# First block of a hybrid encoder layer: four single k-tiles, x split ahead of its weights, h's rows later, and plain units with the rounded halves first

## The chip, the cores and the metric

The kernel runs on one core of one Trainium2 chip. The metric is the device time of one execution in microseconds (us). The median of three runs of the kernel before is 1040.02 us (1039.77 to 1040.2).

The core has five engines with a queue each: TensorE (PE in the profile; its weight loads are PEld), VectorE (DVE), ScalarE (ACT), GpSimd (POOL) and SyncE (SP), which here only issues DMAs. Each engine works through its own queue in order; a semaphore holds an instruction until what it reads is there or the buffer that it writes is free.

## The reference

All in float32: x is 256 tokens by 2048 features, one layer.

```python
xn = rms_norm(h, norm1_g[l])
proj = jnp.einsum('bsd,dn->bsn', xn, w_in[l])
q, k, v, ga, gg = jnp.split(proj, ...)          # 1024, 1024, 1024, 1024, 1024 columns
...                                              # rope, differential attention: att
u = ga * jax.nn.sigmoid(gg)
u = causal_depthwise_conv(u, conv_w[l], conv_b[l])   # 31 taps
u = jax.nn.silu(layer_norm(u, conv_ln_g[l], conv_ln_b[l]))
h = h + jnp.einsum('bsm,md->bsd', jnp.concatenate([att, u], axis=-1), w_out[l])
hn = rms_norm(h, norm2_g[l])
a, bu = hn @ w_gate[l], hn @ w_up[l]             # 5632 columns each
h = h + (jax.nn.silu(a) * bu) @ w_down[l]
```

## The kernel before

**Three products for one.** A float32 matrix product is made of products of rounded halves. Each operand t becomes hi = t rounded to the matmul's type (fp32r) and lo = t - hi, and the product is xhi·whi + xlo·whi + xhi·wlo. ScalarE makes hi (`round_chunk`, L342 for weights; `split_scaled`, L243 for x), VectorE makes lo (`split_chunk`, L351; L244). The token side is the stationary operand, in two halves m of 128 tokens; the weights stream past, 512 columns a matmul.

**Chunks.** The work is one long list `chunks`. A chunk is some k-tiles (128 rows) of a weight matrix; a block is all chunks that add into one pair of accumulators. In the first block a k-tile is 128 x 512 floats, 256 KB, and of x 128 x 256 floats, 128 KB. A chunk normally has two k-tiles; in the first block `XPARTS` (L54) cuts the chunks: before, one, one, then seven of two. `multiply` (L363) runs the 6 matmuls per k-tile: for every k-tile and m the two with whi (L381, L382), then a turn for the side work (`resume`), then all with wlo (L387).

**Order.** The order on each queue is the order in which Python emits the instructions. `run_chunks` (L474) emits for chunk t what is to stand ahead of its matmuls: in the first block the parting (load, rounding, low half) of chunk t + 1, afterwards that of t + 2 and the rounding of t + 3. Loading chunk c first calls `before[c]`, which puts other work ahead of its weights. Four buffers (`raw`, RAW_BUFS) take loaded weights, so SP sends the weights of chunk n + 4 only when chunk n has its low half; four buffers each take the rounded and the low halves.

- x lies transposed in DRAM with the gains in front. Its first k-tile (`head`) and its second are sent by ACT's queue; the rest by `x_load` on SP's, ahead of the weights of the same chunk.
- `x_part` splits x. Before, only that of the first k-tile stands in `before[0]`; the others were emitted by the generator `x_rest` (L532), one part per chunk, at the turn in the middle of chunk t for chunk t + 1. There the cast of chunk t + 1's weights had been emitted already.
- `h_load` sends x's rows (two pieces of 512 KB for each m, 2 MB in all), which are needed for the sum of squares and, much later, the residual. `H_FROM` (L58) is the chunk from which on a piece goes ahead of each chunk's weights: before, the sixth to the ninth.
- After x's parts `x_rest` squares the rows in four groups (L541, L517), and sets `normed`, for which the first block's epilogue `glu_done` (L562) and the late constants (L185) wait.

**Plain units.** The feed-forward products are blocks of two kinds of chunk. A pair of k-tiles goes through seven products instead of eight (`multiply_pair`); the other k-tiles are plain units of two k-tiles (`multiply_two`, L1106): for k-tile i and token half m the products with whi (L1115 with the activations' hi, L1116 with their lo), a turn, then the products with wlo (L1120). The activations' low halves are made by VectorE (`transposed`, L959, for the down projection).

Of the kernel before, what the change touches and what calls it, by code (L numbers as in the profile page):

```python
# [22 lines left out]
NM = S // P  # L23
# [27 lines left out]

WARM = 17

XPARTS = (range(0, 1), range(1, 2)) + tuple(range(k, k + 2) for k in range(2, 16, 2))  # L54

CONV_BLOCKS = (2, 2, 2, 2)

H_FROM = 5  # L58

AHEAD = 2  # L60
ROUND_AHEAD, MINUS_AHEAD = 3, 5
# [53 lines left out]
def tile_block(  # L115
# [40 lines left out]
    def x_load(ks, queue):  # L156
        i, k = divmod(ks[0], HK)
        n = len(ks)
        queue.dma_start(out=halves_of_x[i][:, k : k + n].rearrange("p k s -> p (k s)"),
                        in_=xt[:, NR + ks[0] * S : NR + (ks[0] + n) * S])  # L160
# [24 lines left out]
    def late_constants():  # L185
        late_loads()
        while not normed:
            yield
        yield from lag(16)
        act.mul(cols[:, AT["sg"] : AT["sg"] + 2], cols[:, AT["sg"] : AT["sg"] + 2], 1.0 - LAMBDA_INIT)  # L190

        act.mul(gb[:, 0, :], gb[:, 0, :], 1.0 / math.sqrt(DH))
        hd = DH // 2
        for i, key in enumerate("qk"):
            for m in range(NM):
                t = pre.tile([P, 2, DH], F32, tag=f"gcs{key}{m}", name=f"gcs{key}{m}", bufs=1)
                pool.tensor_tensor(t[:, 0, :], rt[:, m, 0, :], gb[:, i, :], ALU.mult)
                pool.tensor_tensor(t[:, 1, :hd], rt[:, m, 1, :hd], gb[:, i, hd:], ALU.mult)
                pool.tensor_tensor(t[:, 1, hd:], rt[:, m, 1, hd:], gb[:, i, :hd], ALU.mult)
                gcs[key, m] = t  # L200
        lp = pre.tile([P, 2, DH], F32, tag="att", name="lp", bufs=4)
        for i in range(2):
            pool.tensor_tensor(lp[:, i, :], lamv[:, 2 * i, :], lamv[:, 2 * i + 1, :], ALU.mult)
        yield from lag(4)
        dve.tensor_reduce(ls, lp, AX.X, ALU.add)
# [19 lines left out]
    halves = {}  # L225
# [25 lines left out]
    def start(gen):  # L251
        running.append(gen)
# [42 lines left out]
    before = {}  # L295
# [230 lines left out]
    def x_part(ks):  # L526
        for k in ks:
            xT[k] = lhs_pair("x", k)
            src = halves_of_x[k // HK][:, k % HK] if k else head[:, NR:]
            split_scaled(xT[k], src, col("g1", k) if k > 1 else head[:, AT["g1"] + k : AT["g1"] + k + 1])  # L530

    def x_rest():  # L532
        for part in XPARTS[1:]:
            x_part(part)
            yield
            yield
        for c in range(D // N):
            while len(h_loaded) <= c // 2 * NM + 1:
                yield
            for m in range(NM):  # L540
                square_sum(h[m][:, c * N : (c + 1) * N], ss1[m][:, c : c + 1])  # L541
            yield
        for m in range(NM):
            ss = small.tile([P, 1], F32, tag="ss1", name="ss1")
            dve.tensor_reduce(ss, ss1[m], AX.X, ALU.add)
            rsqrt_mean(rstd1[m], ss, D, EPS)
        yield
        normed.append(True)
# [557 lines left out]
    def multiply_two(c):  # L1106
        while not c["ready"](c):
            resume()
        hi, lo, plain = c["hi"], c["lo"], c["plain"](c)
        qs = (Q3, QX) if c["kind"] == "u" else (Q2, Q4)  # L1110

        def first_half(m, i):
            ms = slice(m * P, (m + 1) * P)
            ps = sum_bank(c, qs[m])
            pe.matmul(ps, plain[i][0][:, ms], hi[:, i, :], start=i == 0 and bool(c["first"].get(qs[m])), stop=False)  # L1115
            pe.matmul(ps, plain[i][1][:, ms], hi[:, i, :], start=False, stop=False)  # L1116

        def second_half(m, i):
            ms = slice(m * P, (m + 1) * P)
            pe.matmul(sum_bank(c, qs[m]), plain[i][0][:, ms], lo[:, i, :], start=False,  # L1120
                      stop=i == 1 and bool(c["last"].get(qs[m])))

        if c is chunks[-1]:
            for m in range(NM):
                for half in (first_half, second_half):
                    for i in range(2):
                        half(m, i)
                if m == 0:
                    start(c["done"](c["sums"]))
                    resume()  # L1130
            return
        for i in range(2):
            for m in range(NM):
                first_half(m, i)
        resume()
        for m in range(NM):
            for i in range(2):
                second_half(m, i)
        resume()
        if c["done"]:  # L1140
            start(c["done"](c["sums"]))
# [151 lines left out]
            down_block(g, n)  # L1293
        j0 += nb

    for c, part in enumerate(XPARTS[2:], 2):
        before[c] = lambda part=part: x_load(part, sp)
    before[0] = lambda: (x_part(XPARTS[0]), start(x_rest()))
    for i in range(2 * NM):
        x_first = before.get(H_FROM + i, lambda: None)  # L1300
        before[H_FROM + i] = lambda i=i, x_first=x_first: (x_first(), h_load(i))
    before[len(XPARTS) + 1] = lambda: start(late_constants())
    run_chunks()


# [35 lines left out]
```

## Time and profile before

| | |
|---|---|
| median of three runs | 1040.02 us |
| the profiled execution's own time | 1041.07 us |
| its span, first to last instruction | 1039.2 us |
| granted TensorE clock, mean over the span | 0.998 |
| HBM read, mean rate | 248.80 MB, 247 GB/s with the writes |
| bytes moved in the first 40 us | 14.46 MB, 362 GB/s |
| last matmuls begin / last VectorE work ends | 1034.3 / 1035.7 us |

The profile lists for each engine what it did and what ended its idle time. A line of the view in order of time is: start in us, duration in us, engine, source line, operation, out<-in, shapes, count, and in brackets the idle time before it with what ended it. A line of the waits is: engine, tile and line that waited, what it waited for, us in total, times, longest. In the list of DMA issues, KB are 1024 bytes, and the last number is the us from issue to landing. Matmuls overlap: one is listed with 0.39 us, but the next starts 0.23 us after it, so paces are read from starts. The last 4 us are the epilogue of the last block and its store, which the change does not touch.

### The profile page before, as it was taken

How to read it: one execution, taken by the hardware profiler on the slowest of the kernel's cores; microseconds unless marked ns; L12 is line 12 of the kernel's file. 1: busy time of each engine (PE TensorE's matmuls, PEld its weight loads, DVE VectorE, ACT ScalarE, POOL GpSimd, SP SyncE). 2: the span in 40 equal slices, each digit the busy share in tenths (PEclk: the TensorE clock that was granted, in tenths of full speed). 3: DMA queues.
4: the chain of work that ended last, by engine and by line, in shares of the span. 5: the costliest groups of instructions: out<-in, count | busy, mean ns of one | idle time of the engine just before them, and what ended most of it. 6: DMA issues, size and time to landing. Idle time of an engine off the chain costs nothing.

```text
span 1039.2 us, 13042 instructions
## 1 busy us (share of the span) xinstructions
PE 1030.1 (99%) x4641; PEld 850.3 (82%) x4641; DVE 862.3 (83%) x1086; ACT 685.6 (66%) x864; POOL 155.4 (15%) x198
## 2 busy tenths in 40 slices
PE   8999999999999999999999999999999999999998
PEld 6888888888888888788888888888888888888886
DVE  5599989898546699999978789999896697998983
ACT  5855568766856567777556567776765666767761
POOL 0040133411100101001002120010001121101021
PEclk9999999999999999999999999999999999999999
DMA  9867766676566669898889998987969999879896
GB/s 357 302 202 211 238 206 213 187 211 176 163 201 231 230 215 281 241 323 240 257 246 298 257 306 267 309 229 249 307 187 285 300 271 331 235 243 298 250 249 129
DMA packets 65777, 258.05 MB, mean 248 GB/s; under 512 B 7344, under 2 KB 8624, under 8 KB 58288
## 3 DMA queue, kind: packets, MB, share of 16 engines
q1 hardware_dynamic: 48656, 201.34, 53.5%
q0 software_dynamic: 16768, 55.58, 28.2%
q8 instruction: 36, 0.59, 0.2%
q10 hardware_dynamic: 288, 0.29, 0.1%
q14 instruction: 29, 0.24, 0.1%
HBM read 248.80 MB, written 8.39 MB: 247 GB/s over the span
## 4 chain that ended last, share of the span: by engine, by line
PE 95%; DVE 2%; ACT 1%; issue 1%; DMA 1%; POOL 0%; SPq 0%; DVEq 0%
PE q L1116 11%; PE q L1120 11%; PE q L1115 11%; PE acc L387 11%; PE acc L382 11%; PE acc L381 11%; PE q L1094 9%; PE q L1096 8%; PE q L1095 8%; PE ps_a L922 1%; DMA raw<-in_wts_dram 1%; PE ps_s L731 1%; PE ps_o L809 0%; DVE y L596 0%; PE ps_h L859 0%
## 5 line engine op out<-in xcount | busy, mean ns | idle before, releaser
L342 ACT CAST whi<-raw 128x1024 fp32r<-128x1024 f32 (+1 forms) x261 | 270.3, 1046 | 105.1 <-PE acc L382 42.0
L351 DVE TENSOR_TENSOR wlo<-raw,whi 128x1024 fp32r<-128x1024 f32 (+1 forms) x173 | 209.0, 1218 | 72.9 <-ACT whi L342 71.4
L381 PE MATMUL acc<-whi,lhi 128*128 128x512 f32 x416 | 164.7, 396 | 1.5 <-ACT lhi L243 1.4
L382 PE MATMUL acc<-whi,llo 128*128 128x512 f32 x416 | 162.8, 391 | 0.7 <-DVE llo L244 0.7
L1077 DVE TENSOR_TENSOR wl<-wt,wh 128x2048 fp32r<-128x2048 f32 x58 | 132.7, 2287 | 20.6 <-ACT wh L1072 20.6
L1068 ACT CAST wh<-wb 128x1536 fp32r<-128x1536 f32 x58 | 86.0, 1483 | 87.5 <-PE q L1095 49.1
L346 POOL DMA_DIRECT2D wlo<-in_wts_dram x74 | 65.0, 889 | 510.4 <-ACT wlo L345 483.6
L1115 PE MATMUL q<-whi,chi 128*128 128x512 f32 x320 | 124.7, 390 | 0.0
L1116 PE MATMUL q<-whi,clo 128*128 128x512 f32 x320 | 124.6, 389 | 0.0
L1072 ACT CAST wh<-wt 128x2048 fp32r<-128x2048 f32 x58 | 110.4, 1904 | 18.5 <-DVE wt L1063 18.4
L1094 PE MATMUL q<-wh,fhi 128*128 128x512 f32 x280 | 109.2, 390 | 0.4 <-DVE sum L1199 0.4
L1096 PE MATMUL q<-wl,fhi 128*128 128x512 f32 x280 | 109.0, 389 | 0.0
L1095 PE MATMUL q<-wh,flo 128*128 128x512 f32 x280 | 109.0, 389 | 0.0
L596 DVE SCALAR_TENSOR_TENSOR y<-upad,cw,y 128x256 f32<-128x256 f32 x240 | 100.8, 488 | 5.3 <-ACT y L589 5.3
L1076 DVE TENSOR_TENSOR wl<-wb,wh 128x1536 fp32r<-128x1536 f32 x58 | 101.6, 1752 | 2.3 <-ACT wh L1068 2.3
L387 PE MATMUL acc<-wlo,lhi 128*128 128x512 f32 x368 | 101.4, 397 | 0.2 <-DVE wlo L351 0.2
L381 PEld LDWEIGHTS acc<-whi,lhi 128*128 128x128 f32 x416 | 78.5, 189 | 18.5 <-ACT lhi L243 1.8
L382 PEld LDWEIGHTS acc<-whi,llo 128*128 128x128 f32 x416 | 78.5, 189 | 17.3 <-DVE llo L244 1.2
L1120 PE MATMUL q<-wlo,chi 128*128 128x512 f32 x320 | 86.9, 393 | 0.0
L387 PEld LDWEIGHTS acc<-wlo,lhi 128*128 128x128 f32 x368 | 68.9, 189 | 14.6 <-DVE wlo L351 0.6
L345 ACT ACTIVATE wlo<-raw 128x1024 fp32r<-128x1024 f32 x74 | 78.1, 1056 | 0.0
L1061 DVE TENSOR_TENSOR wt<-wb 128x1024 f32<-128x1024 f32 x58 | 70.8, 1221 | 1.8 <-DMA wb<-in_wts_dram 1.3
(224 smaller groups left out, 1732.5 us busy)
## 6 DMA issues: line engine op xcount, KB each, us to landing
raw<-in_wts_dram SPq DMA_DIRECT2D x259, 512.0 KB, 5.6
wb<-in_wts_dram SPq DMA_DIRECT2D x57, 1024.0 KB, 8.1
wlo<-in_wts_dram POOLq DMA_DIRECT2D x74, 512.0 KB, 9.3
lod<-in_wts_dram POOLq DMA_DIRECT2D x14, 512.0 KB, 5.8
out_dram<-sum POOLq DMA_DIRECT2D x22, 256.0 KB, 7.2
h<-in_x_dram SPq DMA_DIRECT2D x4, 512.0 KB, 8.4
out_dram<-h POOLq DMA_DIRECT2D x8, 256.0 KB, 4.7
xt<-in_xt_dram SPq DMA_DIRECT2D x7, 256.0 KB, 6.9
```

What stands on the lines that cost most here:

```text
L342: act.copy(c["hi"], c["raw"])
L351: dve.tensor_tensor(c["lo"], c["raw"], c["hi"].bitcast(F32), ALU.subtract)
L381: pe.matmul(ps[m], xhi[:, ms], hi[:, j, :], start=c["first"] and j == 0, stop=False)
L382: pe.matmul(ps[m], xlo[:, ms], hi[:, j, :], start=False, stop=False)
L387: pe.matmul(ps[m], xhi[:, ms], lo[:, j, :], start=False, stop=c["last"] and j == nk - 1)
L1077: dve.tensor_tensor(c["lo"][:, :4], c["t"], c["hi"][:, :4].bitcast(F32), ALU.subtract)
L1094: pe.matmul(ps, fhi[:, f, p, :], c["hi"][:, w], start=bool(first), stop=False)
L1095: pe.matmul(ps, flo[:, f, p, :], c["hi"][:, w], start=False, stop=False)
L1096: pe.matmul(ps, fhi[:, f, p, :], c["lo"][:, w], start=False, stop=bool(last))
L1115: pe.matmul(ps, plain[i][0][:, ms], hi[:, i, :], start=i == 0 and bool(c["first"].get(qs[m])), stop=False)
L1116: pe.matmul(ps, plain[i][1][:, ms], hi[:, i, :], start=False, stop=False)
L1120: pe.matmul(sum_bank(c, qs[m]), plain[i][0][:, ms], lo[:, i, :], start=False, stop=i == 1 and bool(c["last"].get(qs[m])))
```

## The change

- `XPARTS` becomes four single k-tiles and six pairs: ten chunks in the first block instead of nine. x's third and fourth k-tile and their weights are loaded, rounded and multiplied singly.
- `x_part` of every chunk moves into `before[c]`: x is split on ScalarE and VectorE ahead of the same chunk's weights, no longer at the turns of `x_rest`.
- h's rows go ahead of chunks 8 to 11 (counted from 0) instead of 5 to 8. `x_rest` starts with the tenth chunk and holds only the squares.
- The late constants start ahead of chunk 12 instead of chunk 10. One chunk of that shift is the new chunk of the first block.
- In `multiply_two` the products of the rounded activations with whi come first for all four (i, m), then those of the low halves. The last chunk of all keeps its order.

```diff
-XPARTS = (range(0, 1), range(1, 2)) + tuple(range(k, k + 2) for k in range(2, 16, 2))
+XPARTS = tuple(range(k, k + 1) for k in range(4)) + tuple(range(k, k + 2) for k in range(4, 16, 2))
...
-H_FROM = 5
+H_FROM = 8
...
     def x_rest():
-        for part in XPARTS[1:]:
-            x_part(part)
-            yield
-            yield
         for c in range(D // N):
...
-        def first_half(m, i):
+        def first_half(m, i, halves=(0, 1)):
             ms = slice(m * P, (m + 1) * P)
             ps = sum_bank(c, qs[m])
-            pe.matmul(ps, plain[i][0][:, ms], hi[:, i, :], start=i == 0 and bool(c["first"].get(qs[m])), stop=False)
-            pe.matmul(ps, plain[i][1][:, ms], hi[:, i, :], start=False, stop=False)
+            for e in halves:
+                pe.matmul(ps, plain[i][e][:, ms], hi[:, i, :], stop=False,
+                          start=i == e == 0 and bool(c["first"].get(qs[m])))
...
-        for i in range(2):
-            for m in range(NM):
-                first_half(m, i)
+        for e in range(2):
+            for i in range(2):
+                for m in range(NM):
+                    first_half(m, i, (e,))
         resume()
...
-    for c, part in enumerate(XPARTS[2:], 2):
-        before[c] = lambda part=part: x_load(part, sp)
-    before[0] = lambda: (x_part(XPARTS[0]), start(x_rest()))
+    for c, part in enumerate(XPARTS):
+        before[c] = lambda c=c, part=part: (x_load(part, sp) if c > 1 else None, x_part(part))
+    before[H_FROM + NM - 1] = lambda part=XPARTS[H_FROM + NM - 1]: (x_load(part, sp), x_part(part), start(x_rest()))
     for i in range(2 * NM):
         x_first = before.get(H_FROM + i, lambda: None)
         before[H_FROM + i] = lambda i=i, x_first=x_first: (x_first(), h_load(i))
-    before[len(XPARTS) + 1] = lambda: start(late_constants())
+    before[H_FROM + 2 * NM] = lambda: start(late_constants())
```

## The prediction

> **What bounds the kernel now.** I read the page first (spans and busy shares), then TensorE's waits, then the first 32 us in order of time, then the DMA landings.
>
> ```profile
> span 1039.2 us, 13042 instructions
> PE 1030.1 (99%) x4641; PEld 850.3 (82%) x4641; DVE 862.3 (83%) x1086; ACT 685.6 (66%) x864; POOL 155.4 (15%) x198
> ```
>
> TensorE is busy for all but 9 us. So only three things can make this kernel shorter: fewer matmuls, a shorter idle time of TensorE, or a better clock. The change keeps the matmuls. The waits name nearly all of the idle time that is not the start or the tail:
>
> ```profile
> PE acc L381 <- ACT lhi L243: 1.4, 1, 1.4
> PE ps_warm L149 <- POOL neghalf L143: 1.4, 1, 1.4
> PE acc L382 <- DVE llo L244: 0.7, 1, 0.7
> PE q L1116 <- DVE llo L959: 0.6, 2, 0.4
> PE q L1094 <- DVE sum L1199: 0.4, 1, 0.4
> PE acc L387 <- DVE wlo L351: 0.2, 1, 0.2
> ```
>
> The change touches three of these rows: L381 and L382 (x's halves late in the first block) and L1116 (an activation's low half late in a plain unit). Together they are 2.7 us. The clock adds to that. Three equal stretches of the first block follow; the columns are length, busy us of PE, PEld, DVE, ACT and POOL with counts, then TensorE's granted clock, DMA share and GB/s:
>
> ```profile
> 5.60:9.00 3.40, 2.95 (x12) 2.00 (x12) 1.45 (x3) 1.26 (x3) 0.00 (x0) 1.00 0.98 372
> 9.00:12.40 3.40, 1.74 (x6) 1.23 (x7) 2.92 (x4) 3.12 (x6) 0.00 (x0) 1.00 1.03 399
> 12.40:15.80 3.40, 3.40 (x9) 2.60 (x8) 3.08 (x6) 1.92 (x4) 0.00 (x0) 0.51 1.01 371
> ```
>
> After a stretch in which PE was busy for 2.95 of 3.40 us the clock stayed at 1.00; after one with 1.74 of 3.40 it was 0.51 for the next 3.40 us. The half clock costs about 1.7 us, which no wait shows. The DMA engines are full (share about 1) throughout: the first block is bound by its feed. These are the matmuls and, below them, ScalarE's work:
>
> ```profile
> 5.38 0.61 PE L381 MATMUL acc<-whi,lhi 128*128 128x512 f32 x1
> ...
> 29.02 0.39 PE L381 MATMUL acc<-whi,lhi 128*128 128x512 f32 x1
> ...
> 31.74 0.39 PE L381 MATMUL acc<-whi,lhi 128*128 128x512 f32 x1
> ```
>
> ```profile
> 4.73 1.12 ACT L342 CAST whi<-raw 128x512 fp32r<-128x512 f32 x2
> 5.76 0.51 ACT L243 ACTIVATE lhi<-xt,head 128x256 fp32r<-128x256 f32 x1
> 8.40 1.04 ACT L342 CAST whi<-raw 128x1024 fp32r<-128x1024 f32 x1 [2.14 <-DMA raw<-in_wts_dram]
> 9.36 0.91 ACT L243 ACTIVATE lhi<-xt,cols 128x256 fp32r<-128x256 f32 x2
> ...
> 15.74 1.05 ACT L342 CAST whi<-raw 128x1024 fp32r<-128x1024 f32 x1 [1.35 <-DMA raw<-in_wts_dram]
> ...
> 25.41 1.05 ACT L342 CAST whi<-raw 128x1024 fp32r<-128x1024 f32 x1 [1.36 <-DMA raw<-in_wts_dram]
> ...
> 28.12 0.62 ACT L517 ACTIVATE junk<-h 128x512 f32<-128x512 f32 x1
> ...
> 31.01 2.93 ACT L342 CAST whi<-raw 128x1024 fp32r<-128x1024 f32 x3
> ```
>
> The last chunk of the first block runs from 29.02 to 31.74: 2.72 us for 12 matmuls, 0.2267 us each. The block has 16 k-tiles of 6 matmuls, so 96 x 0.2267 = 21.76 us at full pace. It takes 31.74 - 5.38 = 26.36. **4.6 us are lost**: 2.1 in the two waits, 1.7 to the clock, and about 0.8 in the first slow matmul and in the starts after the waits. That is the pool from which the first half of the change can draw.
>
> **The change, part by part.** I number chunks as the new kernel does: c0 to c3 one k-tile, c4 to c9 two, c10 the first of the next block; wN is cN's weights. A k-tile of weights is 256 KB, one of x 128 KB, each piece of h's rows 512 KB.
>
> *The feed.* ScalarE's waits on the DMA are landings. From 15.74 to 25.41 three chunks landed with 256 KB of x, 512 of h and 512 of weights each: 3840 KB in 9.67 us, 397 KB per us. From 8.40 to 15.74 it was three chunks' x and weights (3 x 768 KB) and one piece of h: 2816 KB, 384 KB per us. So a landing goes by the bytes issued ahead of it. Counted from the code's order and sizes, the old kernel has issued 797 KB through w1 (x0 with the gains is 157), 1565 through its third chunk (8.40) and 4381 through its sixth (15.74). In the new order w3 ends at the same 1565 KB, so it lands at 8.40. Then w4 (2333) lands at 8.40 + 768/384 = 10.40, w5 at 12.4, w6 at 14.4, w7 at 16.4. The first h comes only ahead of w8: w9 (7197 KB) lands at 15.74 + 2816/397 = 22.83, w10 (8221) at 25.41. That is the same byte order as before with 2048 KB of h moved behind the chunks that were starved.
>
> Does the smaller first load leave the queue empty? w4 needs a raw buffer back:
>
> ```profile
> 6.08 0.33 SPq L333 DMA_DIRECT2D raw<-in_wts_dram  x1
> ```
>
> ```profile
> raw<-in_wts_dram SPq DMA_DIRECT2D x1, 512.0 KB, 3.2
> ```
>
> The first row is when the old fifth weight load went out, once the first chunk's low half was made; w4 will go at the same time. The second is a load in a quiet stretch (56 to 62 us): 3.2 us from issue to landing. 6.08 + 3.2 = 9.3 is earlier than 10.40, so the bytes ahead bind, not the issue. A gap of some tenths is possible.
>
> *Order on ScalarE and VectorE.* Now x's halves are queued ahead of the weights' cast. In the old order x's tiles waited behind the cast of 8.40 although nothing shows them waiting for their own data (9.36 follows the cast at once). A single k-tile costs ScalarE 0.51 + 1.12/2 = 1.07 us against 1.36 us of matmuls, so it keeps up. Two more casts and subtractions in all cost nothing, hidden in ScalarE's waits for the DMA (2.14 and 1.35 in the rows above); without that cover, 2 x 0.1 us. c1 to c3 then run without a wait: w3 at 8.40 gives a cast by 8.97, and c3 is wanted at 5.38 + 1.6 + 2 x 1.36 = 9.7 (c0 takes 1.36 and some 0.25 for its slow first matmul). c4 is wanted at 11.07; its cast ends at 10.40 + 1.05 = 11.45, so **a new wait of 0.45 us**. From then on PE needs 2.72 us per chunk and the feed 768/384 = 2.0, so the lead grows. In the stretch 9.0 to 12.4 PE would be busy for 2.95 of 3.40, the very number after which the clock held: **the half clock goes**.
>
> *h's squares.* ScalarE squares h in groups of four; 28.12 to 31.01 is one group, 2.9 us. In the old program the cast of the next block's first chunk stood ahead of the group; now it stands behind. w9's cast ends at 22.83 + 1.05 = 23.9, the squares at 26.8, c10's cast at 27.8; PE wants c10 at 5.38 + 0.25 + 21.76 + 0.45 = 27.84. So 0 to 0.3 us, I take 0.1. SP also sends h's last pieces, and then the late constants (764 KB by the code's shapes), between the next weight loads: w11 lands at 25.41 + 1024/397 = 28.0 against a start of c11 at 30.6, w12 at 28.0 + 1276/397 = 31.2 against 33.3. Both casts (1.05) fit.
>
> Sum of the first half: c10 starts at 27.9 instead of 31.74, **3.8 us gained** (bounds: 4.4 with no new wait, 2.5 with the new wait at 1.7).
>
> *Plain units.* Four matmuls with the rounded halves come ahead of the four with the low halves. The two waits of L1116 in order of time, and VectorE beside them:
>
> ```profile
> 984.52 0.48 PE L1115 MATMUL q<-whi,lhi 128*128 128x512 f32 x1
> 985.37 0.50 PE L1116 MATMUL q<-whi,llo 128*128 128x512 f32 x1 [0.38 <-DVE llo L959]
> ...
> 987.99 0.39 PE L1115 MATMUL q<-whi,lhi 128*128 128x512 f32 x1
> ...
> 990.29 1.07 PE L1120 MATMUL q<-wlo,lhi 128*128 128x512 f32 x4
> ```
>
> ```profile
> 984.63 0.69 DVE L959 TENSOR_TENSOR llo<-ac,lhi 128x512 fp32r<-128x512 f32 x1
> ...
> 987.83 0.69 DVE L959 TENSOR_TENSOR llo<-ac,lhi 128x512 fp32r<-128x512 f32 x1
> 988.43 1.22 DVE L351 TENSOR_TENSOR wlo<-raw,whi 128x1024 fp32r<-128x1024 f32 x1
> ```
>
> The first low half is there at 985.32; four rounded matmuls last to 984.52 + 0.91 = 985.43: no wait. The second is late by VectorE's own queue: 988.52, and the weights' low half at 989.65, so L1120 starts at 989.7 instead of 990.29: what is late next is that subtraction. **0.6 us gained** (0.57 by the waits, 0.75 if VectorE moves up too). The other units show no wait and keep their count of matmuls; they change accumulators after each matmul instead of after two, which the rows price at nothing (bounds 0 and 0.01 us a unit).
>
> *Does the gain reach the end?* VectorE is the only other engine that is full later, while the convolution's taps run:
>
> ```profile
> DVE t L708 <- ACT qn L701: 2.7, 1, 2.7
> ```
>
> This is its one wait between 147 and 170 us, on a chain that starts at a matmul's result. So VectorE had 2.7 us to spare and moves with PE. I take the whole gain.
>
> Sum: 3.8 + 0.6 = 4.4 us from the profiled execution's own 1041.07 gives 1036.7; the median of the runs is 1.05 lower, 1040.02, and **1035.6** there.
>
> **The rivals.**
>
> *The half clock stays.* By the Trainium skill, "TensorE: Matmul & The Clock Gate", Part 1, the gate looks through a free-running window of about 3.4 us and throttles after an idle one. No run here shows an idle window before the drop: PE was busy for 1.74 of 3.40. By that rule the stall would not be the cause. If the drop is not tied to that stall, or if w4 is a microsecond late (1.95 of 3.40 busy, near the 1.74 that dropped), 1.7 us of the gain stay away, in the second case 1.0 more: 1037.3 to 1038.3. For: the threshold lies anywhere between 1.74 and 2.95. Against: 2.95 held.
>
> *The conv stage takes it back.* The 0.2 us wait at L387 for wlo says VectorE was once just in time. If its run were paced by itself alone, PE would wait there for all of the 3.8 us: 1039.4. The 2.7 us wait above speaks against it.
>
> *Each transfer pays its fixed time in series.* 512 KB at 397 KB per us is 1.3 of the quiet row's 3.2 us; 1.9 is fixed. Two more transfers now lie ahead of w4 for the same bytes: w4 at 14.2, c4 at 15.3, the clock halved once more: c10 at 33.4, 1.7 later than before; less 0.6 that is 1041.1. The Trainium skill, "DMA: Bandwidth & Descriptors", section Bandwidth, speaks for this and against the change: transfers should be gathered to 1 MiB, and these are cut to 128 and 256 KB. Against: 3840 KB in nine transfers of 256 and 512 KB went at full rate, so the fixed time overlaps.
>
> *The feed stays slow (slower).* x1's row and its issue:
>
> ```profile
> 1.16 0.46 ACTq L159 DMA_DIRECT2D xt<-in_xt_dram  x1
> ```
>
> ```profile
> xt<-in_xt_dram ACTq DMA_DIRECT2D x1, 128.0 KB, 4.1
> ```
>
> It landed at 5.26 with 797 KB issued through w1; the third chunk at 8.40 with 1565: only 245 KB per us. If short rows keep that pace through w9, it lands at 5.26 + 6400/245 = 31.4; cast, squares and c10's cast follow on ScalarE (1.05 + 2.9 + 1.05), so c10 starts at 36.4, 4.7 late; less 0.6: 1044.1. It decides once w9 lands after 27.4, a mean below 290 KB per us. Against: from w4 on rows are as long as before, and those went at 384 and more.
>
> **How the numbers follow.** A run of this kernel can be told from no change from about 0.2% on, 2.1 us. Forecast 0.70; the half clock stays 0.14 (0.10 of it still past 0.2%); taken back 0.06; fixed times 0.05; slow feed 0.05. Faster 0.70 + 0.10 = 0.80, same 0.04 + 0.06 + 0.05 = 0.15, slower 0.05. The range runs from 1034.8 (no new wait, 0.75 in the plain units) to 1038.3 (the worse end of the half clock); it leaves out 0.16.
>
> **What would show it.** The first matmul of the second block at 27.9 (27.4 to 29); the clock at 1.00 in all stretches of the first block; no L381 wait on lhi and no L382 wait on llo, one of about 0.4 on w4's cast near 11 us; L1116 waiting for llo under 0.5 us in all; the last matmuls 4.4 us earlier and the same waits between. A clock of 0.5 anywhere, a wait at c10 over 1 us, or a longer wlo wait near 165 us would show the prediction wrong at that step.

## The result and the profile after

| | median, us | lowest to highest | executions |
|---|---|---|---|
| before | 1040.03 | 1039.77 to 1040.84 | 12 |
| changed | 1037.70 | 1037.16 to 1038.38 | 12 |

The changed kernel takes 0.9978 of the time before (95% interval 0.9969 to 0.9987), **2.33 us less**; 1035.6 was forecast, 4.4 less. Its profiled execution took 1037.66 us (span 1035.9), 3.41 less than the one of before (1041.07). Removed lines shift the numbers of the later ones: L955 and L592 are the old L959 and L596, L1117 is the old L1120, and L1112 stands for both old L1115 and L1116. The whole waits of TensorE come first:

```profile
PE ps_warm L149 <- POOL neghalf L143: 1.4, 1, 1.4
PE acc L381 <- ACT whi L342: 1.2, 2, 0.8
PE acc L387 <- DVE wlo L351: 0.5, 1, 0.5
PE q L1090 <- DVE sum L1197: 0.4, 1, 0.4
PE q L1112 <- DVE llo L955: 0.2, 1, 0.2
```

The rows of x's halves (1.4 and 0.7 us) are gone, and the one of the plain units fell from 0.6 to 0.2. A wait for w4's cast has come (0.84; the other 0.34 is the start), and the wait for wlo in the convolution's stretch went from 0.2 to 0.5. The three stretches of the first block:

```profile
5.60:9.00 3.40, 3.40 (x16) 2.78 (x17) 3.40 (x7) 3.40 (x8) 0.00 (x0) 1.00 0.91 306
9.00:12.40 3.40, 2.56 (x12) 1.83 (x11) 1.31 (x4) 1.48 (x4) 0.00 (x0) 1.00 0.97 324
12.40:15.80 3.40, 3.40 (x16) 2.79 (x15) 3.40 (x6) 2.79 (x5) 0.00 (x0) 1.00 1.00 394
```

The clock stays at 1.00 after a stretch with 2.56 of 3.40 us busy, where before it fell after one with 1.74. The last column is new, too: 306 and 324 GB/s where the kernel before had 372 and 399. TensorE and ScalarE in order of time:

```profile
5.46 0.50 PE L381 MATMUL acc<-whi,lhi 128*128 128x512 f32 x1 [0.34 <-ACT whi L342]
...
12.03 0.50 PE L381 MATMUL acc<-whi,lhi 128*128 128x512 f32 x1 [0.84 <-ACT whi L342]
...
25.79 0.39 PE L381 MATMUL acc<-whi,lhi 128*128 128x512 f32 x1
...
28.72 0.50 PE L381 MATMUL acc<-whi,lhi 128*128 128x512 f32 x1
```

```profile
10.93 1.05 ACT L342 CAST whi<-raw 128x1024 fp32r<-128x1024 f32 x1 [1.93 <-DMA raw<-in_wts_dram]
...
15.37 1.06 ACT L342 CAST whi<-raw 128x1024 fp32r<-128x1024 f32 x1 [0.43 <-DMA raw<-in_wts_dram]
...
23.79 1.05 ACT L342 CAST whi<-raw 128x1024 fp32r<-128x1024 f32 x1 [1.37 <-DMA raw<-in_wts_dram]
...
27.64 1.03 ACT L342 CAST whi<-raw 128x1024 fp32r<-128x1024 f32 x1
...
43.29 1.06 ACT L337 ACTIVATE lod<-raw 128x1024 fp32r<-128x1024 f32 x1 [1.01 <-DMA raw<-in_wts_dram]
44.25 1.03 ACT L342 CAST whi<-raw 128x1024 fp32r<-128x1024 f32 x1
45.19 0.58 ACT L581 COPY upad<-ps_u 128x512 f32<-128x512 f32 x1
```

The casts at 10.93, 15.37, 23.79 and 27.64 are those of w4, w6, w9 and w10. c10 starts at 28.72, not at 31.74 as before (3.02 earlier) and not at 27.9 as forecast. The plain units at the same place as before:

```profile
981.90 1.18 PE L1112 MATMUL q<-whi,lhi 128*128 128x512 f32 x4
...
985.98 1.21 PE L1112 MATMUL q<-whi,llo 128*128 128x512 f32 x4 [0.18 <-DVE llo L955]
987.03 1.09 PE L1117 MATMUL q<-wlo,lhi 128*128 128x512 f32 x4
```

TensorE is 984.52 - 981.90 = 2.62 us ahead of the kernel before when the units begin, and 990.29 - 987.03 = 3.26 at L1117. So the trace splits the 3.26 us in three: 3.02 gained in the first block, 0.40 given back on the way, 0.64 gained in the plain units.

**Where the 0.40 is given back.** It is the convolution's stretch. VectorE's taps begin once ScalarE has copied the convolution's input (`upad`, L581), which TensorE transposes first (L580). The copy and the taps before, then the transposes and the taps of the changed kernel:

```profile
47.79 0.59 ACT L585 COPY upad<-ps_u 128x512 f32<-128x512 f32 x1 [2.10 <-PE ps_u L584]
```

```profile
49.54 0.88 DVE L596 SCALAR_TENSOR_TENSOR y<-upad,cw,y 128x256 f32<-128x256 f32 x2 [5.32 <-ACT y L589]
```

```profile
44.28 0.60 PE L580 MATMUL ps_u<-ident,u 128*128 128x128 f32 x4
```

```profile
46.93 1.68 DVE L592 SCALAR_TENSOR_TENSOR y<-upad,cw,y 128x256 f32<-128x256 f32 x4 [3.21 <-ACT y L585]
```

The transposes start 2.88 us earlier (47.16 to 44.28), so 0.14 is lost ahead of them. Before, the copy followed them at once. Now they end at 44.88 and the copy starts at 45.19, behind the cast of 44.25 and the `lod` copy of 43.29 (for some later chunks a transfer makes the weights' low half, from this copy), which had waited 1.01 us for its data. The taps begin at 46.93 instead of 49.54: 2.61 earlier, 0.41 less than c10. From there VectorE runs with one gap, of 1.1 us in both kernels, to the end of three subtractions. That run, and GpSimd beside it, first in the kernel before and then in the changed one:

```profile
125.35 3.51 DVE L351 TENSOR_TENSOR wlo<-raw,whi 128x1024 fp32r<-128x1024 f32 x3
131.63 0.69 DVE L708 TENSOR_TENSOR t<-qn,gcsk 128x512 f32<-128x512 f32 x1 [2.76 <-ACT qn L701]
```

```profile
125.68 3.25 POOL L220 TENSOR_SCALAR rsq<-ssq 128x4 f32<-128x4 f32 x1 [10.73 <-ACT junk L517]
```

```profile
122.80 3.49 DVE L351 TENSOR_TENSOR wlo<-raw,whi 128x1024 fp32r<-128x1024 f32 x3
129.06 0.69 DVE L704 TENSOR_TENSOR t<-qn,gcsk 128x512 f32<-128x512 f32 x1 [2.77 <-ACT qn L697]
```

```profile
122.82 3.53 POOL L220 TENSOR_SCALAR rsq<-ssq 128x4 f32<-128x4 f32 x1 [10.72 <-ACT junk L517]
...
127.93 0.19 POOL L220 TENSOR_SCALAR rsq<-ssq 128x4 f32<-128x4 f32 x1
```

The same small GpSimd instruction (L220) takes 0.19 us alone and 3.25 or 3.53 us beside VectorE's run, and ends 0.07 and 0.06 us after it (128.93 against 128.86; 126.35 against 126.29). In all 14 profiles of this study it ends 0.05 to 0.07 us after VectorE's run, though it begins from 0.26 us before the three subtractions to 1.03 after their start and so lasts 2.51 to 3.83. The chain goes on from GpSimd to ScalarE's qn and back to VectorE. So the 2.7 us in which VectorE waits there are no spare time: the chain that it waits for began when VectorE itself paused. By the Trainium skill, "SBUF — State Buffer", section "Who interferes with whom", a VectorE instruction with two inputs in SBUF holds the read port that GpSimd's reads need; the trace agrees, and shows GpSimd let in only after the third of three such instructions. VectorE was thus 2.57 us earlier here (131.63 to 129.06), TensorE 2.86 (its low products, 125.22 to 122.36), and the difference of 0.3 is what the wlo wait grew by:

```profile
163.40 1.21 PE L387 MATMUL acc<-wlo,lhi 128*128 128x512 f32 x4 [0.47 <-DVE wlo L351]
```

### The profile page after: what moved, and what is told of

Same layout as the page of the kernel before. It is cut to its first block, busy times and chain, and to the rows that moved or that the text cites. A ratio compares the mean times of both kernels' runs of the same rounds, so it can differ in the third digit from the quotient of the medians.

```text
span 1035.9 us, 13050 instructions
## 1 busy us (share of the span) xinstructions
PE 1028.0 (99%) x4641; PEld 849.0 (82%) x4641; DVE 862.7 (83%) x1087; ACT 685.8 (66%) x865; POOL 155.1 (15%) x198
## 4 chain that ended last, share of the span: by engine, by line
PE 83%; DVE 9%; DMA 3%; POOL 2%; ACT 1%; issue 1%; DVEq 0%; ACTq 0%
PE q L1112 23%; PE q L1117 12%; PE q L1090 9%; PE q L1091 9%; PE q L1092 9%; PE acc L387 6%; PE acc L381 6%; PE acc L382 6%; DVE y L592 5%; DVE wlo L351 3%; DMA raw<-in_wts_dram 3%; PE ps_a L918 1%; POOL rsq L220 1%; PE ps_s L727 1%; PE ps_o L805 1%
## 5 line engine op out<-in xcount | busy, mean ns | idle before, releaser
L382 PE MATMUL acc<-whi,llo 128*128 128x512 f32 x416 | 162.2, 390 | 0.0
L592 DVE SCALAR_TENSOR_TENSOR y<-upad,cw,y 128x256 f32<-128x256 f32 x240 | 100.5, 481 | 3.2 <-ACT y L585 3.2
L382 PEld LDWEIGHTS acc<-whi,llo 128*128 128x128 f32 x416 | 78.2, 188 | 16.0
L1117 PE MATMUL q<-wlo,chi 128*128 128x512 f32 x320 | 86.9, 393 | 0.0
L1112 PE MATMUL q<-whi,chi 128*128 128x512 f32 x320 | 85.8, 390 | 0.0
L1112 PE MATMUL q<-whi,clo 128*128 128x512 f32 x320 | 85.6, 389 | 0.0
```

The lines of the kernel that those rows point to most:

```text
L382: pe.matmul(ps[m], xlo[:, ms], hi[:, j, :], start=False, stop=False)
L592: dve.scalar_tensor_tensor(y[:, ct, :], src, wk, y[:, ct, :], ALU.mult, ALU.add)
L1112: pe.matmul(ps, plain[i][e][:, ms], hi[:, i, :], stop=False, start=i == e == 0 and bool(c["first"].get(qs[m])))
```

## The experiments

The twelve kernels ran in three groups of four, in the order of the table; each group shared a chip and the executions of the kernel before (medians there 1040.08, 1040.42 and 1040.12). Gains are told against these medians. The intervals of h_late_alone, singles_alone, plain_alone and filler include no change, so what they say rests on their traces more than on their times.

| label | from | median, us | lowest to highest (n) | ratio to before, 95% interval |
|---|---|---|---|---|
| x_first_alone | before | 1039.17 | 1038.67 to 1039.61 (11) | 0.9989 [0.9980, 0.9998] |
| h_late_alone | before | 1039.00 | 1038.02 to 1040.90 (11) | 0.9992 [0.9984, 1.0001] |
| singles_alone | before | 1041.06 | 1040.51 to 1041.43 (11) | 1.0008 [0.9999, 1.0017] |
| plain_alone | before | 1039.66 | 1038.97 to 1040.24 (11) | 0.9995 [0.9986, 1.0004] |
| no_singles | changed | 1037.19 | 1036.54 to 1038.34 (6) | 0.9970 [0.9958, 0.9981] |
| h_early | changed | 1041.68 | 1041.14 to 1042.72 (11) | 1.0012 [1.0004, 1.0021] |
| shared_raw | changed | 1036.89 | 1036.54 to 1037.57 (5) | 0.9967 [0.9955, 0.9980] |
| filler | before | 1040.77 | 1040.50 to 1041.12 (11) | 1.0003 [0.9994, 1.0012] |
| minus_later | changed | 1037.66 | 1036.14 to 1039.29 (11) | 0.9978 [0.9969, 0.9986] |
| shared_minus | changed | 1036.30 | 1035.90 to 1036.72 (5) | 0.9963 [0.9951, 0.9976] |
| all_three | changed | 1036.68 | 1036.29 to 1037.57 (5) | 0.9968 [0.9955, 0.9980] |
| after_again | changed, unaltered | 1037.55 | 1036.97 to 1038.97 (11) | 0.9974 [0.9965, 0.9983] |

### Each part alone

**x split ahead of its weights**, with h's place and the chunks as before:

```diff
     def x_rest():
-        for part in XPARTS[1:]:
-            x_part(part)
-            yield
-            yield
+        yield
+        yield
...
-    for c, part in enumerate(XPARTS[2:], 2):
-        before[c] = lambda part=part: x_load(part, sp)
-    before[0] = lambda: (x_part(XPARTS[0]), start(x_rest()))
+    for c, part in enumerate(XPARTS):
+        before[c] = lambda c=c, part=part: (x_load(part, sp) if c > 1 else None, x_part(part))
+    before[8] = lambda part=XPARTS[8]: (x_load(part, sp), x_part(part), start(x_rest()))
```

> The kernel before with x's split ahead of the same chunk's weights and nothing else (chunks of 1, 1, 2, ..., h from the sixth chunk; the squares at the same turns as before). Cast-order theory: x's third and fourth k-tiles lie in memory while the cast waits for its weights until 8.40, so the two waits on lhi and llo go, the third chunk runs from about 9.55 without a gap, the stretch 9.0 to 12.4 is busy for about 2.9 us and the half clock goes: second block begins 1.6 us earlier without the clock's part, about 3.0 with it, at 28.7 to 30.2. Median 1037.5 to 1038.6. Feed-order theory (the gain is the bytes of h moved back and the smaller first loads): the third chunk still waits for its weights at 8.40, so under 1 us is gained, 1039.2 or more.

It gained 0.91 us, at the edge of the feed-order theory's forecast. The waits for x's halves go, as the other theory has it, and waits for the weights' cast take their place:

```profile
PE acc L381 <- ACT whi L342: 1.4, 4, 0.8
```

Its third chunk starts at 9.11 instead of 9.91 and its second block at 29.12 instead of 31.74, inside the cast-order forecast. Of these 2.62 us 2.10 reach the taps and 2.16 the end of the profiled execution (1038.91 against 1041.07). The median gained less, as the profiled execution of before is 0.99 above the median of that kernel in this group; why is said under the next run.

**h's rows two chunks later**, all else as before:

```diff
-H_FROM = 5
+H_FROM = 7
...
-    before[len(XPARTS) + 1] = lambda: start(late_constants())
+    before[H_FROM + 2 * NM] = lambda: start(late_constants())
```

> The kernel before with h's rows two chunks later (behind as many k-tiles as in the change) and nothing else. Cast-order theory: the third and fourth chunk's weights are ahead of h in the old order too, so the waits and the half clock stay, and the later chunks had no waits: 1040.0 within 0.4. Feed-order theory: less in front of the weights, 1 to 2 us gained, 1038 to 1039.

The median gained 1.08 us, as the feed-order theory forecast, while the waits for x's halves stayed (1.4 and 0.7), as the other theory has it. The executions fall into two groups: eight at a mean clock of 0.999 to 1.000 (1038.02 to 1039.16, median 1038.89), three at 0.998 (1040.43 to 1040.90). The profiled one is of the second group:

```profile
9.00:12.40 3.40, 1.75 (x4) 1.25 (x5) 2.92 (x4) 3.11 (x6) 0.00 (x0) 0.81 1.04 413
12.40:15.80 3.40, 3.40 (x12) 2.66 (x12) 3.38 (x7) 3.31 (x6) 0.00 (x0) 0.69 1.03 398
```

The half clock is there only in some executions, and here it costs 2.0 us (1040.89 against 1038.89), all that the later h gains and more. The kernel before has it, too: of its 76 executions in the three groups 24 had a mean clock of 0.998, with a median of 1040.82, and 52 a higher one, with 1040.00. There it costs 0.8, since TensorE without it only meets the late feed sooner. **The profiled execution of before, on which the prediction was built, was of that kind** (0.998, 1041.07). The moment at which full clock begins varies, too: between 4.3 and 7.5 us by the clock records of the 14 traces. By the Trainium skill, "TensorE: Matmul & The Clock Gate", Part 1, the gate looks through a free-running window; the spread agrees with that. That a window must be idle does not: the drop followed stretches that were about half busy.

The traces suggest what decides. Both profiles with a half clock had it for 3.41 us, and it began 6.83 us, twice 3.41, after full clock had: 5.65 to 12.48 before, 4.26 to 11.09 here. Counted in spans of 3.41 us from the start of full clock, TensorE was busy for 1.82 and 1.33 us of the span that ended with the drop. The least busy spans of the first block after which the clock held have 1.98 (singles_alone), 2.33 (plain_alone) and 2.45 (filler). So whether a stall drops the clock may hang on where such a span falls on it; no trace of an execution of before without the drop is there to show it.

**Four single k-tiles**, with x's halves as before and h one chunk later as the new chunk asks:

```diff
-XPARTS = (range(0, 1), range(1, 2)) + tuple(range(k, k + 2) for k in range(2, 16, 2))
+XPARTS = tuple(range(k, k + 1) for k in range(4)) + tuple(range(k, k + 2) for k in range(4, 16, 2))
...
-H_FROM = 5
+H_FROM = 6
```

> The kernel before with four single k-tiles and nothing else (h's rows ahead of the same k-tiles as before). Cast-order theory: the stall moves from the third chunk to the fifth, whose x is split only after a cast that lands at 10.4 to 10.9; its low half comes 2.5 us after the fourth chunk ends, and the clock falls as before. Second block at 31 to 32, median 1039.5 to 1040.3. Feed-order theory: the first four k-tiles run through, only the wait for the fifth chunk's weights is left, second block at 29 or earlier, median 1038.0 or less.

0.98 us longer, more than either theory forecast. Its second block starts at 31.88, and two of its waits say why: x's halves stand behind more casts.

```profile
PE acc L382 <- DVE llo L244: 1.6, 5, 0.7
...
PE acc L381 <- ACT lhi L243: 0.7, 1, 0.7
```

**Plain units alone** (the part of the diff in `multiply_two`):

```diff
-        for i in range(2):
-            for m in range(NM):
-                first_half(m, i)
+        for e in range(2):
+            for i in range(2):
+                for m in range(NM):
+                    first_half(m, i, (e,))
```

> The kernel before with the plain units' order of the change and nothing else. By the two waits near 985 and VectorE's next subtraction 0.6 us gained: median 1039.4, L1116's waits under 0.25 us in all. If changing accumulators after each matmul costs something, the gain is missing: 1040.0 or more, and the plain units take more than 2.72 us each.

The median gained 0.42 of the 0.6 expected, and the waits at L1116 fell by 0.4:

```profile
PE acc L382 <- DVE llo L244: 1.1, 3, 0.7
...
PE q L1116 <- DVE llo L959: 0.2, 1, 0.2
```

This profiled execution had no half clock, and the first block of this kernel is that of before: its second block starts at 31.05, so the two differ by 0.69 us of c10's 31.74. That is not the price of the half clock alone: here full clock began only at 7.5 us, which slowed the first chunk and cut the wait for lhi to 0.3, and the wait at L382 grew to 1.1 (0.7 before).

The three parts that gain sum to 2.41 us; the whole change gained 2.33 and 2.57.

### What the parts do together

**The changed kernel without the single k-tiles:**

```diff
-XPARTS = tuple(range(k, k + 1) for k in range(4)) + tuple(range(k, k + 2) for k in range(4, 16, 2))
+XPARTS = (range(0, 1), range(1, 2)) + tuple(range(k, k + 2) for k in range(2, 16, 2))
...
-H_FROM = 8
+H_FROM = 7
```

> The change without its single k-tiles: chunks of 1, 1, 2, 2, ... as before, x ahead of its weights, h as many bytes later as in the change, plain units as in the change. If the parts add up, alone they gave 0.9 (x first), 1.1 (h late) and 0.4 us (plain units), together 2.4, and the singles nothing: 1037.4 to 1038.0, the same as the change. If the singles are what makes x first pay, at least 0.6 us is missing: 1038.3 or more, with a wait of 0.8 us or more ahead of the third chunk and some runs at half clock.

1037.19, not above the changed kernel: the single k-tiles bring nothing that can be measured. What goes with them is in the DMA columns (share, GB/s):

```profile
5.60:9.00 3.40, 3.40 (x12) 2.46 (x12) 2.37 (x5) 2.13 (x5) 0.00 (x0) 1.00 0.97 353
9.00:12.40 3.40, 2.82 (x13) 2.29 (x13) 2.76 (x4) 3.28 (x6) 0.00 (x0) 1.00 1.04 416
```

In the first stretch that is 353/0.97 = 364 GB/s at full share against 306/0.91 = 336 with the singles, in the second 416/1.04 = 400 against 324/0.97 = 334. Over all profiles the first stretch gives 364 to 380 per full share in the six kernels without the four singles and 305 to 352 in the eight with them.

**h's rows early again**, x still first:

```diff
-H_FROM = 8
+H_FROM = 6
...
-    before[H_FROM + NM - 1] = lambda part=XPARTS[H_FROM + NM - 1]: (x_load(part, sp), x_part(part), start(x_rest()))
+    before[9] = lambda part=XPARTS[9]: (x_load(part, sp), x_part(part), start(x_rest()))
...
-    before[H_FROM + 2 * NM] = lambda: start(late_constants())
+    before[12] = lambda: start(late_constants())
```

> The change with h's rows ahead of the same k-tiles as before (chunks 6 to 9 instead of 8 to 11), everything else as changed. Feed theory: each h puts 512 KB, 1.3 us, ahead of the seventh to tenth chunk's weights, which then land at about 16.1, 19.3, 22.5 and 25.8; the waits for the casts add up to about 1 us by the second block: 1038.5 to 1039.2. If only the order on ScalarE counts, h's place is worth nothing: 1037.5 to 1037.9.

1041.68: the whole gain and 1.3 us more are gone, far more than expected.

```profile
PE acc L381 <- ACT whi L342: 2.5, 6, 0.8
...
PE acc L381 <- ACT v L789: 1.0, 1, 1.0
```

```profile
17.54 0.50 PE L381 MATMUL acc<-whi,lhi 128*128 128x512 f32 x1 [0.25 <-ACT whi L342]
...
24.02 0.50 PE L381 MATMUL acc<-whi,lhi 128*128 128x512 f32 x1 [0.23 <-ACT whi L342]
27.23 0.50 PE L381 MATMUL acc<-whi,lhi 128*128 128x512 f32 x1 [0.20 <-ACT whi L342]
31.06 0.50 PE L381 MATMUL acc<-whi,lhi 128*128 128x512 f32 x1 [0.77 <-ACT whi L342]
```

With a piece of h in each, chunks come every 3.24 us: 1280 KB at 395 KB per us, while TensorE needs 2.72. Once x is out of the way the place of h is what the first block's time hangs on. Another 1.0 us of waiting came later, for `v` (L789), and at 200 us nothing is left of the 2.15 us by which its taps start earlier than before; why wasn't followed up.

**Two single k-tiles in one raw buffer**, so that SP sends w4 sooner:

```diff
+    two_raw = [None]
+
     def load_chunk(c):
...
+        elif c["nk"] == 1:
+            k = c["k0"]
+            if k % 2 == 0:
+                two_raw[0] = wp.tile([P, NK * N], F32, tag="raw", name="raw", bufs=RAW_BUFS)
+            c["raw"] = two_raw[0].rearrange("p (k n) -> p k n", n=N)[:, k % 2 : k % 2 + 1]
```

> The change with two single k-tiles to a raw buffer, so that the fifth chunk's weights can be sent when x's second k-tile has landed (near 5.3) and not when the first low half is made (6.15). If the issue binds their landing, it comes at 10.1 to 10.4 instead of 10.9, and the wait ahead of the fifth chunk falls from 0.84 to under 0.4 us; if the bytes ahead bind, 10.9 and 0.84 stay. In both cases, by the theory that VectorE's taps pace the time up to 163 us and start behind ScalarE's wait for a load near 43 us, the total gains 0 to 0.4 us: 1037.2 to 1037.7. If nothing gives it back, 0.5 to 0.8 us less: 1036.9 to 1037.2.

w4 went out at 4.50 instead of 6.15, 1.65 us earlier. Its cast started 0.38 earlier and the one of w6 0.91, w6's without a wait for data:

```profile
10.55 1.05 ACT L349 CAST whi<-raw 128x1024 fp32r<-128x1024 f32 x1 [1.35 <-DMA raw<-in_wts_dram]
...
14.46 1.05 ACT L349 CAST whi<-raw 128x1024 fp32r<-128x1024 f32 x1
```

```profile
9.00:12.40 3.40, 3.00 (x13) 2.18 (x13) 1.55 (x3) 2.05 (x4) 0.00 (x0) 1.00 1.04 414
```

0.24 us of that this execution had already at ScalarE's first instruction on x (4.14 against 4.38). The first stretch stays at 324 GB/s, the second rises from 324 to 414. So w4's own landing follows its issue by a quarter at most, but most of w6's lateness goes with the earlier issue. Four single k-tiles hold all four raw buffers with 1024 KB of weights, where the first four chunks of before held 1536. The wait at c4 fell to 0.4 us, the second block started at 28.10, and the median is 1036.89; of the 3.64 us at c10 3.63 reach the taps, so nothing was given back.

**Filler.** The kernel before with 14 transposes between its second and third chunk, so that TensorE is busy while it would wait:

```diff
             chunks[t]["multiply"](chunks[t])
+            if t == 1:
+                warm_up(14)
```

> The kernel before with 14 more transposes of the identity on TensorE between the second and the third chunk, where it stalls (their result is not used). If the half clock answers to that stall, no run is left with a mean clock of 0.998 or less, where 9 of 33 runs of the kernel before had one, and these runs' 1040.4 to 1041.2 go: median 1039.8, none above 1040.4. If the clock's drop has nothing to do with the stall, a quarter of the runs keeps it.

```profile
9.00:12.40 3.40, 2.88 (x18) 2.31 (x17) 3.29 (x5) 3.13 (x7) 0.00 (x0) 1.00 1.04 413
```

None of its 11 executions had a mean clock under 0.999, where the kernel before in the same group had 8 of 22. So the stall is what drops the clock. Yet nothing is gained (1040.77 where 1039.8 was expected): the fourth chunk starts at 13.41 instead of 14.96, but the last chunk's matmuls with llo wait until 28.75 for their data, and the second block starts at 31.38. With the clock kept, TensorE waits for the feed instead. That these executions take 0.5 us more than those of before without the half clock in the same group (median 1040.24) is not explained.

### Where the gain goes behind the first block

**The lod copy four chunks ahead** instead of five:

```diff
-ROUND_AHEAD, MINUS_AHEAD = 3, 5
+ROUND_AHEAD, MINUS_AHEAD = 3, 4
```

> The changed kernel with one edit: the difference raw - whi that a transfer makes for some later chunks (the ScalarE copy into lod) starts four chunks ahead instead of five. Theory (the taps' start sets what survives): near 43 us ScalarE no longer waits 1.0 us for that chunk's landing, so the copy of the convolution's input (45.19 us) starts when the transposes are done, 0.3 to 0.5 us sooner, VectorE's taps move by as much, TensorE's wait for wlo near 163 us falls from 0.47 to 0.2 or less, and the time is 0.3 to 0.4 us below the changed kernel's. Rival (what is lost is lost in the first block alone): the taps start sooner but the time is the same within 0.1 us. Second rival: the difference now arrives late for its chunk, a wait at L387 of over 0.3 us appears, and the time is the same or longer.

The same time as the changed kernel, 1037.66. Of its waits the new one, then ScalarE:

```profile
PE acc L387 <- DMA lod<-in_wts_dram: 0.7, 1, 0.7
```

```profile
45.06 0.59 ACT L581 COPY upad<-ps_u 128x512 f32<-128x512 f32 x1 [2.11 <-PE ps_u L580]
```

The copy now waits for its transposes alone. c10 is 2.87 earlier than before and the transposes and the taps 2.73, so the 0.14 ahead of the transposes is still lost, the 0.27 at the copy is not, and the wlo wait is gone. In its place stands the second rival: at 160.57 us a matmul waits 0.7 us for a `lod`. One wait was traded for another, and the time alone doesn't tell the theories apart.

**Both: shared raw buffers and the later lod copy.**

```diff
-ROUND_AHEAD, MINUS_AHEAD = 3, 5
+ROUND_AHEAD, MINUS_AHEAD = 3, 4
...
+    two_raw = [None]
+
     def load_chunk(c):
...
+        elif c["nk"] == 1:
+            k = c["k0"]
+            if k % 2 == 0:
+                two_raw[0] = wp.tile([P, NK * N], F32, tag="raw", name="raw", bufs=RAW_BUFS)
+            c["raw"] = two_raw[0].rearrange("p (k n) -> p k n", n=N)[:, k % 2 : k % 2 + 1]
```

> The changed kernel with two edits: each pair of single k-tiles shares one raw buffer (as in the earlier run of that alone, 1036.89), and the lod copy starts four chunks ahead instead of five. Theory (landing by bytes, then the taps' start): both gains are there side by side, the taps start 1.0 us sooner by the buffers and 0.2 to 0.5 more by the copy; 1036.4 to 1036.8. Rival (the feed's next limit takes it): no better than the buffers alone, 1036.9 to 1037.2.

1036.30, and each of its five executions (1035.90 to 1036.72) is below each of the eleven of the unaltered changed kernel in the same group (1036.97 to 1038.97). It is the fastest version of the study, 0.9963 of before.

```profile
PE acc L388 <- ACT whi L349: 0.7, 2, 0.4
```

No wait for wlo or lod is left. The taps start 3.84 us earlier than before and c10 3.93.

**The squares one chunk's turn later as well** (on top of the two edits above):

```diff
     def x_rest():
+        yield
+        yield
         for c in range(D // N):
```

> As the run with the shared raw buffers and the later lod copy, and h's squares one chunk's turn later, so that the cast of the second block's first chunk stands ahead of ScalarE's first group of squares. By the prediction's step on the squares (0.1 to 0.3 us of waiting at that chunk) it gains 0.1 to 0.3 us more: 1036.2 to 1036.6. Rival: the squares' later end delays the first block's epilogue and with it the taps' start, and the time is 0.2 or more above that run's.

1036.68, with overlapping ranges. The first block has no wait at all in its profile, but in that execution full clock came only at 7.5 us: the first chunk took 2.50 us (c1 starts at 7.73, c0 at 5.23) where the run above took 1.51. Between c10 and the taps it lost 0.31 us, where the run above lost 0.09, which speaks for the rival; its median is 0.38 above. Whether the squares' place is worth anything is left open.

**The changed kernel again:**

> The changed kernel unaltered, so that the other runs of this call are compared with it on the same chip: 1037.2 to 1038.2, 0.9978 of the kernel before (0.9969 to 0.9987); no execution with a mean clock under 0.999.

1037.55. The profiled execution was its slowest (1038.97) and shows what varies from one to the next:

```profile
24.87 1.05 ACT L342 CAST whi<-raw 128x1024 fp32r<-128x1024 f32 x1 [1.40 <-DMA raw<-in_wts_dram]
...
28.71 1.03 ACT L342 CAST whi<-raw 128x1024 fp32r<-128x1024 f32 x1
```

```profile
29.80 0.50 PE L381 MATMUL acc<-whi,lhi 128*128 128x512 f32 x1 [0.81 <-ACT whi L342]
```

w9 came 1.08 us later than in the first profile, the four squares stand between its cast and c10's, and c10 waited 0.81.

How far the first block's gain arrives can be read from all runs. The table gives how much earlier than in the profile of before (us) c10 starts, the taps start, and the 801st matmul into `acc`, the early blocks' accumulators (near 200 us), starts:

| | c10 | taps | near 200 us |
|---|---|---|---|
| x_first_alone | 2.62 | 2.10 | 2.13 |
| h_late_alone | 0.10 | 0.09 | 0.05 |
| singles_alone | -0.14 | -0.15 | -0.19 |
| plain_alone | 0.69 | 0.69 | 0.66 |
| filler | 0.36 | 0.36 | 0.33 |
| changed | 3.02 | 2.61 | 2.55 |
| after_again | 1.94 | 1.18 | 1.18 |
| no_singles | 2.82 | 2.65 | 2.67 |
| shared_raw | 3.64 | 3.63 | 3.63 |
| shared_minus | 3.93 | 3.84 | 4.03 |
| all_three | 3.60 | 3.29 | 3.54 |
| minus_later (lod late) | 2.87 | 2.73 | 2.19 |
| h_early (v late) | 0.68 | 2.15 | -0.15 |

Four kernels without a new wait have c10 and taps that differ by 0.3 or more and so tell the two apart. In three of them (x_first_alone, changed, after_again) what is left at 200 us is what the taps' start had, within 0.1, and not what TensorE had at c10. all_three has 3.54, nearer to its c10; that was not followed.

## Why the prediction was right in its direction and about twice too large in its size

The forecast was 4.4 us, 2.33 came. Step by step:

- **x's two waits go, c1 to c3 run without one: right.** No wait on lhi or llo in the first block.
- **"the half clock goes": right, but it was not worth 1.7 us.** No execution of the changed kernel (23) had a mean clock under 0.999. The step that failed is the pool: "4.6 us are lost" was read from one execution, and the clock's 1.7 us were put down to every one. Two thirds of the executions of before have no half clock, the median among them, and in the others it costs 0.8 us. Taking the "1.05 lower" median as a fixed offset kept the half clock in a median that hadn't got it; between the two profiled executions the gain was 3.41. **About 0.7 to 0.8 us** of the miss: 1040.82 against 1040.00 by the executions, 31.74 against 31.05 by the profiles.
- **"w4 (2333) lands at 8.40 + 768/384 = 10.40": 0.53 late, and w6 0.97 late** (its cast, after a wait for data, at 15.37 against 14.4). The steps that failed are "a landing goes by the bytes issued ahead of it" and "the bytes ahead bind, not the issue". w3, for which 8.40 was read from the same bytes, was cast at 7.59 already. With w4 sent 1.65 us sooner, w6's cast started 0.91 sooner (0.24 of it that execution had from the start). The third rival (small transfers) has the right sign, a lower rate with the singles in the first stretch and not a fixed time of each in series. But shared buffers leave that stretch at 324 GB/s and still bring w6 nearly back to its forecast, by the next stretch's 414 instead of 324; so the size of the transfers alone is not the cause. Nor is the issue alone: without the singles the fifth weight load went out at 6.03, and that stretch had 416. Why the two together slow it stays open. The new wait was 0.84 instead of 0.45.
- **"0 to 0.3 us, I take 0.1" for the squares:** 0.2 in the first profile (28.72 against 25.79 + 2.72 = 28.51), 0.81 in the second. w9 was late by 0.96 in the first (23.79 against 22.83) and by 2.04 in the second. The bound was too narrow, as it rested on one landing. With the wait at c4 and the slower first matmuls behind it (2.87 us for that chunk instead of 2.72) this makes c10's 28.72 instead of 27.9: **0.8 us** of the miss.
- **"So VectorE had 2.7 us to spare and moves with PE. I take the whole gain.": wrong**, by **0.4 us**. The chain that VectorE waits for passes GpSimd, which could not finish while VectorE ran, so the wait moves with VectorE. VectorE's run begins with the taps, and those began 2.61 us earlier, not 3.02. The second rival named the right place (paced by itself) with too high a price. That ScalarE's in-order queue holds the taps' start is shown by the run with the later lod copy (0.14 lost instead of 0.41; where the 0.14 goes ahead of the transposes was not followed); that GpSimd's block ties VectorE to itself rests on the ends of the instructions in all profiles, and no run removed it.
- **Plain units, 0.6: right**, 0.64 in the trace, and what came next was late VectorE work, as written. It wasn't the weights' low half but still llo, by 0.18.

The three misses make 0.75 + 0.8 + 0.4 = 1.95 of the 2.07 us that were not gained; beside them, 1041.07 was 0.25 above the median of its kind (1040.82). The rivals that would have made the kernel slower did not occur.

## What to carry to other kernels

Before a loss is put into a pool, see whether it is in the median execution: the mean clock of each execution tells it without a second profile. An engine's wait is spare time only if the chain that it waits for doesn't run through something that the engine itself holds up; follow it to its first step. In a block that is bound by its feed, look first for large loads that nobody needs yet (h's place was worth 3.5 to 4 us once x stood first, 1.0 of it in a later wait), and only then cut the first tiles smaller, and see that the small tiles do not take the buffers on which the next loads wait.

## What the runs showed of the hardware that was not expected

- The granted clock at the start differs between executions of one kernel: full clock came between 4.3 and 7.5 us, and a stall as in the kernel before dropped it in 24 of 76 executions. In the two traces with a drop it came 6.83 us after full clock, held for 3.41, and followed spans of 3.41 us with 1.82 and 1.33 busy; 1.98 held.
- A GpSimd instruction of 0.19 us lasted 2.51 to 3.83 us beside three subtractions of VectorE and ended 0.05 to 0.07 us after them, in 14 of 14 profiles.
- Between 5.6 and 9.0 us the DMA engines moved 305 to 352 GB/s per full share in the kernels with four single k-tiles (loads of 256 KB of weights, 128 KB of x) and 364 to 380 in those without. Between 9.0 and 12.4 us it was 334 to 363 in the five of the former whose fifth weight load went out at 6.1 us, and 395 to 398 in the three in which it went out at 4.5.
